# Two stacked transformer blocks on one core: modulation from transposed weights on VectorE, row broadcasts as transposes, float32 gate products over four row strips

## The chip, the cores and the metric

One Trainium2 chip, one of its cores. The metric is the device time of one execution in microseconds (us), the median of several runs of the kernel. The trace is of one more execution, taken by the hardware profiler. Engine names in the rows: PE is TensorE's matmuls, PEld its weight loads, DVE is VectorE, ACT is ScalarE, POOL is GpSimd, SP is SyncE, which issues most DMAs.

## The reference, cut to what matters

The kernel computes two blocks one after the other over a sequence of 512 tokens with 1024 columns. The first block is an FFN, a mixer (attention and a state-space part), a second FFN and a gated per-layer embedding (PLE). The second block has two layers; each modulates its input by a condition vector, runs two recurrent branches (RG-LRU and mLSTM) and projects back. What the change touches:

```python
def rms_norm(x, g):      # in every stage: one factor per token
    return x * lax.rsqrt(jnp.mean(x * x, axis=-1, keepdims=True) + EPS) * g

c_act = jax.nn.silu(c)                                    # (1, 1024)
for l in range(DEPTH_2):                                  # two layers
    mod = c_act @ w_ada[l] + b_ada[l]                     # (1, 3072)
    shift, scale, gate = jnp.split(mod, 3, axis=-1)
    h = rms_norm(x, norm_g[l]) * (1.0 + scale[:, None, :]) + shift[:, None, :]
    ...
    gates = (jnp.concatenate([q, k, v], axis=-1) @ w_if + b_if)   # in the mLSTM branch: 8 gate rows
    ...
    h = h * lax.rsqrt(jnp.mean(h * h, axis=-1, keepdims=True) + EPS)   # per head of 256 columns
    ...
    x = x + gate[:, None, :] * y
```

All of it is in float32.

## The kernel before, in words

Activations lie transposed: a tile is 128 columns of the model by 512 tokens, so a matrix of 1024 columns is eight tiles. Big matmuls take float32 numbers as a high and a low part and add three products (`mm3`, lines 125 to 127). Weights stream from memory in chunks of eight 128 x 128 blocks, in the order of use (`Stream`); each chunk is loaded by SP, its high part is copied by ScalarE (line 96) and its low part subtracted by VectorE (line 98), up to two chunks ahead. The program writes out the order of the work on each engine by hand; engines run their own instructions in order and wait for each other by semaphores.

*Row broadcasts.* A norm has one factor per token, and tokens lie along the free axis. `Norm.colsums` (line 165) sums squares over partitions with matmuls against ones, `rsqrt` (lines 207 to 214) computes the factors on VectorE as a column `col` of 128 x 4, and `Norm.part2` turns that column into a 128 x 512 tile with the factors repeated on all partitions (line 195): four matmuls, the column broadcast as the stationary operand and the identity `k.ident` as the moving one. ScalarE copies the result to SBUF (line 199). There are eight such norms. In each mLSTM head, `head_f2` does the same with the head's factors (line 1737) and VectorE multiplies two tiles by it (line 1740): four heads in each of two layers. The attention part already has transposes by TensorE (line 1023, eight of them, float32, 128 x 128).

*Modulation.* `second_prepare` makes a list of steps, each with a planned cost in us, for work that isn't needed until the second block. `Fill.grant` pops steps from that list whenever the second FFN has issued a stretch of its matmuls: 5.2 us x 0.26 of credit for each of the 44 projections, and a share after most output tiles. `silu_c` loads the condition vector as 128 x 8 and applies silu. For each layer 24 loads (`load`, 512 KB each, on SP's queue, three buffers) and 24 steps `acc` follow: VectorE multiplies the weights by the condition and adds up over the eight row blocks, four instructions over 256 columns per step (lines 1223 and 1225), into the tile `adaa` of 128 x 12 x 256. `colsum` then adds up over partitions with eight one-column matmuls against ones (line 1232), three times per layer. For layer 0 these calls are steps of the list as well; for layer 1 they are kept in `k.tail` and issued by `ple` after its last projection (`tail[0]`), by `between` before and after the broadcast of the norm in front of layer 0 (`tail[1]`, `tail[2]`), and `tail[3]` adds the bias behind the modulated tiles. `fold` (line 1245) prepares weights for the gates in the same list.

*Between PLE and layer 0.* `between` computes the norm, broadcasts it, and `modulate` makes the eight input tiles of the layer: a product with the row (lines 1350 and 1352), scale and shift on ScalarE (line 1359, high part) and VectorE (line 1360), and the low part (line 1363). Layer 1 starts by `renorm` in the same way.

*Gate products.* In `layer`, `gate_mm` (line 1479) adds the products for the eight mLSTM gates into one PSUM bank `G`, in strips of 32 rows. Per head, `qkv` issues four products of float32 parts (F32R, from `L.gvr`) into strip 0 and, after the head's q, k and v projections, four float32 products (two of q, two of k). The float32 ones go round strips 1, 2, 3 by their number `n`, sixteen in a layer. `gates1` adds the strips up with `sel8`, which has ones in every strip.

Of the kernel before, what the change touches and what calls it, by code (L numbers as in the profile page):

```python
# [129 lines left out]
class Norm:  # L130
# [60 lines left out]
    def part2(self):  # L191
        k, nc = self.k, self.k.nc
        pb = k.ps.tile([128, T], F32, name="pm", bufs=2)
        for j in range(4):
            nc.tensor.matmul(pb[:, j * 128:(j + 1) * 128], self.col[:, j:j + 1].to_broadcast([128, 128]),  # L195
                             k.ident, start=True, stop=True)
        self.wide = pb
        self.row = k.work.tile([128, T], F32, name="nrow", bufs=1)
        nc.scalar.activation(self.row, pb, AF.Copy)
# [977 lines left out]
def second_prepare(k, pool, ins):  # L1177

    nc, v = k.nc, k.nc.vector
    steps = []  # L1180
    k.lay = [Ctx() for _ in range(2)]
    c = pool.tile([128, 8], F32, name="b2c")
    th = pool.tile([128, 8], F32, name="b2cth")

    def silu_c():
        nc.sync.dma_start(c, ins["cvec"])
        nc.scalar.activation(th, c, AF.Tanh, scale=0.5)
        v.tensor_scalar(th, th, 0.5, 0.5, op0=OP.mult, op1=OP.add)
        v.tensor_mul(c, c, th)
    steps.append((0.4, silu_c))  # L1190

    for l in range(2):
        L = k.lay[l]
        L.mod = k.const2.tile([128, 24], F32, name=f"mod{l}")
        L.gs = k.const2.tile([128, 8], F32, name=f"gs{l}")
        L.sp = k.const2.tile([128, 2, 8], F32, name=f"sp{l}")
        L.hg = k.const2.tile([128, 8], F32, name=f"hg{l}")
        L.gv = k.const2.tile([128, 8, 32], F32, name=f"gv{l}")
        L.gvr = k.const2.tile([128, 8, 32], F32R, name=f"gvr{l}")
        L.wif = k.const2.tile([128, 24, 32], F32, name=f"wif{l}")  # L1200
        L.bif = k.const2.tile([128, 8], F32, name=f"bif{l}")
        L.v = lambda name, l=l: k.vec[:, VEC[f"{name}.{l}"][0]:VEC[f"{name}.{l}"][0] + VEC[f"{name}.{l}"][1]]

        def loads(L=L, l=l):
            nc.sync.dma_start(L.wif, ins["wif"][l])
            nc.sync.dma_start(L.bif, ins["bif"][l])
            nc.gpsimd.memset(L.gv, 0.0)
        steps.append((0.1, loads))

        boxes, box = {}, {}  # L1210

        def load(i, l=l, boxes=boxes):
            boxes[i] = pool.tile([128, 4, 256], F32, name="adaw", bufs=3)
            nc.sync.dma_start(boxes[i], ins["wada"][l, i // 2, :, i % 2 * 4:i % 2 * 4 + 4])

        def acc(i, boxes=boxes, box=box):
            if i == 0:
                box["a"] = pool.tile([128, 12, 256], F32, name="adaa")
            a, w = box["a"][:, i // 2], boxes[i]
            for d in range(4):  # L1220
                cd = c[:, i % 2 * 4 + d:i % 2 * 4 + d + 1]
                if i % 2 or d:
                    v.scalar_tensor_tensor(a, w[:, d], cd, a, op0=OP.mult, op1=OP.add)  # L1223
                else:
                    v.tensor_scalar(a, w[:, d], cd, None, op0=OP.mult)

        def colsum(n, L=L, box=box):

            if n == 0:
                L.mps = k.ps.tile([128, T], F32, name="pc", bufs=2)  # L1230
            for j in range(8 * n, 8 * n + 8):
                nc.tensor.matmul(L.mps[:, j:j + 1], box["a"][:, j // 2, j % 2 * 128:j % 2 * 128 + 128], k.ones[:, :1],
                                 start=True, stop=True)

        def wload(n, l=l, box=box):
            box["wv"] = pool.tile([128, 2, 2, 256], F32, name="wvt")
            nc.sync.dma_start(box["wv"], ins["wvt"][l, 2 * n:2 * n + 2].rearrange("h p a b -> p h a b"))

        def fold(n, L=L, box=box):
            ps = k.ps.tile([128, T], F32, name="pc", bufs=2)  # L1240
            for h in range(2):
                for di in range(2):
                    i = 2 * h + di
                    for do in range(2):
                        nc.tensor.matmul(ps[:, i * 8:i * 8 + 8], box["wv"][:, h, do, di * 128:(di + 1) * 128],
                                         L.wif[:, 16 + 4 * n + 2 * h + do, 0:8], start=do == 0, stop=do == 1)
            v.tensor_copy(L.gv[:, 4 * n:4 * n + 4, 0:8], ps[:, 0:32].rearrange("p (a b) -> p a b", b=8))
            if n:
                nc.scalar.activation(L.gvr, L.gv, AF.Copy)
                v.tensor_sub(L.gvr[:, :, 8:16], L.gv[:, :, 0:8], L.gvr[:, :, 0:8].bitcast(F32))  # L1250

        step = lambda cost, f, *a: steps.append((cost, lambda: f(*a)))
        for i in range(3):
            step(0.1, load, i)
        step(0.1, wload, 0)
        for i in range(24):
            step(1.4, acc, i)
            if i < 21:
                step(0.1, load, i + 3)
            if l == 0 and i in (9, 17):  # L1260
                step(0.1, colsum, i // 16)
            if i % 12 == 7:
                step(0.3, fold, i // 12)
                if i < 12:
                    step(0.1, wload, 1)

        def mods(L=L):
            v.tensor_add(L.mod, L.mps[:, 0:24], L.v("b_ada"))
            v.scalar_tensor_tensor(L.gs, L.mod[:, 8:16], 1.0, L.v("norm_g"), op0=OP.add, op1=OP.mult)
            v.tensor_scalar(L.hg, L.v("ml_norm_g"), 0.5, None, op0=OP.mult)  # L1270
        if l == 0:
            step(0.3, lambda: None)
            step(0.1, colsum, 2)
            steps.append((0.6, mods))
        else:
            k.tail = [lambda n=n: colsum(n) for n in range(3)] + [mods]

        def sp1(L=L, box=box):
            n, t = (pool.tile([128, 8], F32, name=f"spl{x}", bufs=2) for x in "ab")
            lam = L.v("rg_lambda")  # L1280
            v.tensor_scalar(n, lam, -1.0, None, op0=OP.mult)
            v.tensor_tensor(t, n, lam, op=OP.min)
            v.tensor_scalar(n, n, 0.0, None, op0=OP.max)
            nc.scalar.activation(t, t, AF.Exp)
            box["n"], box["t"] = n, t

        def sp2(L=L, box=box):
            o = pool.tile([128, 8], F32, name="splo")
            log1p_small(k, pool, box["t"], o, [128, 8], "spl1")
            v.tensor_add(o, o, box["n"])  # L1290
            v.tensor_scalar(L.sp[:, 0], o, 4.0, None, op0=OP.mult)
            v.tensor_scalar(L.sp[:, 1], o, -8.0, None, op0=OP.mult)
        steps += [(0.3, sp1), (2.0, sp2)]
    return steps


def ple(k, pool, xs, norm, pt, on_tile, early):
# [35 lines left out]
        if m:  # L1333
            gate1(m, pgs[m])
    proj(7)
    k.tail[0]()
    gate2(7, pps[7])
    early()

# [31 lines left out]
def between(k, scr, nf, ng):  # L1371
# [10 lines left out]
    v.scalar_tensor_tensor(ms, nf.ms, 1e-6, ng.ms, op0=OP.mult, op1=OP.add)  # L1382
    ng.col = k.work.tile([128, 4], F32, name="ncol", bufs=2)
    rsqrt(k, ng.col, ms)
    k.tail[1]()
    ng.part2()
    k.tail[2]()
    xs = modulate(k, 0, ng, gg, scr)
    k.tail[3]()
    rsqrt(k, nf.col, nf.ms)  # L1390

    def root():
# [19 lines left out]
def layer(k, l, xs, aside, ins, scr, norm):  # L1412
# [4 lines left out]
    with ExitStack() as st:  # L1417
# [55 lines left out]

        def gate_mm(w, x):

            parts = x.dtype == F32R
            n = ng[parts]
            g = 0 if parts else 1 + n % 3
            nc.tensor.matmul(G[g * 32:g * 32 + 32], w, x, start=n < (1 if parts else 3),
                             stop=n >= (15 if parts else 13), tile_position=None)  # L1480
            ng[parts] += 1

        def high(src, name):
# [249 lines left out]
        def head_f2(h):  # L1733
            r = S.pop(("r", h))
            ps = k.ps.tile([128, T], F32, name="pc", bufs=2)
            for t in range(4):
                nc.tensor.matmul(ps[:, t * 128:(t + 1) * 128], r[:, t:t + 1].to_broadcast([128, 128]), k.ident,
                                 start=True, stop=True)
            for m in (2 * h, 2 * h + 1):
                v.tensor_mul(n2[m], n2[m], ps)  # L1740

# [313 lines left out]
def pack(inputs, order):  # L2055
# [58 lines left out]
            a = g[n + "_2"][l]  # L2114
            mats[f"{n}.{l}"] = a.reshape(DM, a.shape[-1])
    A["pT"] = c(g["p"][0, 0].T)
    A["cvec"] = c(g["c_2"][0].reshape(8, 128).T)
    A["wada"] = c(g["w_ada_2"].reshape(2, 8, 128, 12, 256).transpose(0, 3, 2, 1, 4))
    wif = np.zeros((2, 128, 24, 32), np.float32)
    wif[..., :8] = g["ml_w_if_2"].reshape(2, 24, 128, 8).transpose(0, 2, 1, 3)  # L2120
    A["wif"] = wif
# [23 lines left out]
    "xT": (DM, T), "vecs": (128, NV), "ident": (128, 128), "wpack": (NCHUNKS, 128, CH * 128),  # L2145
    "rope": (128, 2, T), "s5n": (128, 3, 32), "s5q": (128, 3, 128), "s5cst": (128, 16),
    "s5bn": (128, 2, 512), "s5cn": (128, 2, 512), "s5bq": (8, 128, 2, 256), "s5d": (16, 32),
    "pT": (256, T), "cvec": (128, 8), "wada": (2, 12, 128, 8, 256), "wif": (2, 128, 24, 32), "bif": (2, 128, 8),
    "wvt": (2, 4, 128, 2, 256), "onehot": (8, 4, 128), "osgn": (8, 2), "sel8": (128, 8),
    "cpe": (128, 2, 16), "cw2": (128, 2, 2, 128), "ii": (124, 64), "cmask": (128, 4, 2, 32), "bglu": (128, 4),  # L2150
}
# [21 lines left out]
```

## Time and profile before

| what | value |
|---|---|
| median of 3 runs | 2014.44 us (2013.72 to 2014.51) |
| the profiled execution | 2013.55 us |
| its span, first to last instruction | 2011.8 us |
| mean granted TensorE clock | 0.98 of 2.4 GHz |
| TensorE matmuls busy | 1957.6 us, 97% of the span |
| VectorE busy | 1335.3 us, 66% |
| ScalarE busy | 815.5 us, 41% |
| bytes moved by DMA | 239.59 MB, mean 119 GB/s |

Busy time is the share of the span in which an engine worked on an instruction. A granted clock of 1.0 is TensorE's 2.4 GHz and 0.5 is 1.2 GHz; a value between is a mean over a stretch with both. A row of the timeline gives the start within the span, the length, the engine, the line of the kernel, the operation, what is written from what, and how many instructions of that kind followed each other; matmul lengths overlap, so the distance between starts tells what one costs in a stream. A float32 matmul that isn't a transpose stands in the trace as two instructions.

### The profile page before, as it was taken

How to read it: one execution, taken by the hardware profiler on the slowest of the kernel's cores; microseconds unless marked ns; L12 is line 12 of the kernel's file. 1: busy time of each engine (PE TensorE's matmuls, PEld its weight loads, DVE VectorE, ACT ScalarE, POOL GpSimd, SP SyncE). 2: the span in 40 equal slices, each digit the busy share in tenths (PEclk: the TensorE clock that was granted, in tenths of full speed). 3: DMA queues.
4: the chain of work that ended last, by engine and by line, in shares of the span. 5: the costliest groups of instructions: out<-in, count | busy, mean ns of one | idle time of the engine just before them, and what ended most of it. 6: DMA issues, size and time to landing. Idle time of an engine off the chain costs nothing. (4 is left out here: it accounts for less than half of the span.)

```text
span 2011.8 us, 24981 instructions
## 1 busy us (share of the span) xinstructions
PE 1957.6 (97%) x9432; PEld 1603.7 (80%) x9432; DVE 1335.3 (66%) x2241; ACT 815.5 (41%) x1227; POOL 161.7 (8%) x219
## 2 busy tenths in 40 slices
PE   8999999997999999999999999999999899999997
PEld 6888888886767888888888787888888677888886
DVE  7766576678655577667666775877753765777733
ACT  5323233435554332323244355555532454455521
POOL 1000000210242100000001100110000100101000
PEclk9999999998999999999999799999999899999998
DMA  5334545455201455364532143222242142232241
GB/s 186 102 117 156 160 130 154 162 189 163 90 7 37 155 183 194 118 224 168 168 104 88 45 152 115 71 88 84 74 147 95 63 157 95 74 95 84 81 139 53
DMA packets 100377, 239.59 MB, mean 119 GB/s; under 512 B 24600, under 2 KB 35608, under 8 KB 100256
## 3 DMA queue, kind: packets, MB, share of 16 engines
q1 hardware_dynamic: 100112, 237.82, 36.4%
q8 instruction: 74, 1.21, 0.2%
q14 instruction: 47, 0.39, 0.1%
q10 hardware_dynamic: 144, 0.17, 0.0%
HBM read 215.67 MB, written 21.10 MB: 118 GB/s over the span
## 5 line engine op out<-in xcount | busy, mean ns | idle before, releaser
L98 DVE TENSOR_TENSOR wlo<-wstage,whi 128x1024 fp32r<-128x1024 f32 (+1 forms) x305 | 376.0, 1240 | 149.4 <-ACT whi L96 148.9
L96 ACT ACTIVATE whi<-wstage 128x1024 fp32r<-128x1024 f32 (+1 forms) x306 | 313.5, 1043 | 142.8 <-PE pasecond L126 36.1
L277 ACT ACTIVATE t<-t 128x512 f32<-128x512 f32 x44 | 27.8, 632 | 176.9 <-DVE t L276 176.9
L1223 DVE SCALAR_TENSOR_TENSOR adaa<-adaw,b2c,adaa 128x256 f32<-128x256 f32 x168 | 81.3, 484 | 5.1
L127 PE MATMUL pahead<-xnh,wlo 128*128 128x512 f32 x208 | 81.4, 391 | 2.8 <-DVE wlo L98 2.8
L125 PE MATMUL pahead<-xnh,whi 128*128 128x512 f32 x208 | 83.4, 401 | 0.0
L153 POOL TENSOR_TENSOR nacc<-nacc,nsq 128x512 f32<-128x512 f32 x20 | 26.8, 1342 | 682.0 <-ACT nsq L149 682.0
L126 PE MATMUL pahead<-xnl,whi 128*128 128x512 f32 x208 | 81.0, 390 | 0.0
L125 PE MATMUL pbhead<-xnh,whi 128*128 128x512 f32 x192 | 77.6, 404 | 0.0
L125 PE MATMUL pbfirst<-xnh,whi 128*128 128x512 f32 x176 | 70.4, 400 | 7.1 <-ACT whi L96 6.5
L126 PE MATMUL pbhead<-xnl,whi 128*128 128x512 f32 x192 | 76.0, 396 | 0.0
L127 PE MATMUL pbhead<-xnh,wlo 128*128 128x512 f32 x192 | 76.0, 396 | 0.0
L1454 DVE SCALAR_TENSOR_TENSOR conv<-cpad,vec,conv 128x512 f32<-128x512 f32 x96 | 72.2, 752 | 5.6
L126 PE MATMUL pbfirst<-xnl,whi 128*128 128x512 f32 x176 | 69.6, 395 | 0.3 <-DVE xnl L223 0.3
L127 PE MATMUL pbfirst<-xnh,wlo 128*128 128x512 f32 x176 | 69.1, 393 | 0.0
L125 PE MATMUL pasecond<-xnh,whi 128*128 128x512 f32 x176 | 69.0, 392 | 0.0
L125 PE MATMUL pbsecond<-xnh,whi 128*128 128x512 f32 x176 | 68.8, 391 | 0.0
L125 PE MATMUL pafirst<-xnh,whi 128*128 128x512 f32 x176 | 68.7, 390 | 0.0
L127 PE MATMUL pafirst<-xnh,wlo 128*128 128x512 f32 x176 | 68.6, 390 | 0.0
L127 PE MATMUL pasecond<-xnh,wlo 128*128 128x512 f32 x176 | 68.6, 390 | 0.0
L126 PE MATMUL pafirst<-xnl,whi 128*128 128x512 f32 x176 | 68.5, 389 | 0.0
L127 PE MATMUL pbsecond<-xnh,wlo 128*128 128x512 f32 x176 | 68.5, 389 | 0.0
(754 smaller groups left out, 5266.7 us busy)
## 6 DMA issues: line engine op xcount, KB each, us to landing
wstage<-in_wpack_dram SPq DMA_DIRECT2D x304, 512.0 KB, 3.7
adaw<-in_wada_dram SPq DMA_DIRECT2D x48, 512.0 KB, 4.8
scr_v<-vv SPq DMA_DIRECT2D x16, 256.0 KB, 2.1
vr<-scr_v SPq DMA_DIRECT2D x16, 256.0 KB, 4.4
xr<-scr_x SPq DMA_DIRECT2D x16, 256.0 KB, 5.9
h<-in_xT_dram SPq DMA_DIRECT2D x8, 256.0 KB, 5.8
s5vw<-scr_wq SPq DMA_DIRECT2D x64, 32.0 KB, 2.0
s5vb<-in_s5bq_dram SPq DMA_DIRECT2D x8, 256.0 KB, 2.7
```

Of the source, the lines that this page charges most:

```text
L96: k.nc.scalar.activation(hi[:, s], st[:, s], AF.Copy)
L98: eng.tensor_sub(lo[:, s], st[:, s], hi[:, s].bitcast(F32))
L125: mm(ps, w[0], x[0], start=start, stop=False)
L126: mm(ps, w[0], x[1], start=False, stop=False)
L127: mm(ps, w[1], x[0], start=False, stop=stop)
L153: k.nc.gpsimd.tensor_add(self.acc[1], self.acc[1], sq)
L277: nc.scalar.activation(t1, t1, AF.Silu)
L1223: v.scalar_tensor_tensor(a, w[:, d], cd, a, op0=OP.mult, op1=OP.add)
L1454: v.scalar_tensor_tensor(c, xp[:, 1 + j:1 + j + T], w(j), c, op0=OP.mult, op1=OP.add)
```

## The change

Three things, in one edit:

1. `second_prepare` loads the condition vector as a row of 1024 on all 128 partitions and applies silu to all of it. The modulation weights are laid out transposed on the host: a load brings 128 output columns (as partitions) by 1024 inputs, 512 KB as before. `acc` becomes one `tensor_tensor_reduce`: product with the condition, sum along the free axis, starting from the bias, into one column of `L.mod`; the products themselves go to a tile that nobody reads. `colsum` goes, with the calls in the list, in `ple` and in `between`; `mods` loses its addition and becomes a step of the list for both layers.
2. The row broadcasts of `part2` and `head_f2` are `transpose` calls with the same operands.
3. The float32 gate products go round strips 0 to 3. Strip 0 then holds them on top of the F32R products, so only the first F32R product starts that strip.

```diff
@@ Norm.part2 @@
-            nc.tensor.matmul(pb[:, j * 128:(j + 1) * 128], self.col[:, j:j + 1].to_broadcast([128, 128]),
-                             k.ident, start=True, stop=True)
+            nc.tensor.transpose(pb[:, j * 128:(j + 1) * 128], self.col[:, j:j + 1].to_broadcast([128, 128]), k.ident)
@@ second_prepare @@
-    c = pool.tile([128, 8], F32, name="b2c")
-    th = pool.tile([128, 8], F32, name="b2cth")
+    c = pool.tile([128, DM], F32, name="b2c")
+    th = pool.tile([128, DM], F32, name="b2cth")
 
     def silu_c():
-        nc.sync.dma_start(c, ins["cvec"])
+        src = ins["cvec"]
+        nc.sync.dma_start(c, bass.AP(tensor=src.tensor, offset=src.offset, ap=[[0, 128], [1, DM]]))
...
-    steps.append((0.4, silu_c))
+    steps.append((2.4, silu_c))
...
         def load(i, l=l, boxes=boxes):
-            boxes[i] = pool.tile([128, 4, 256], F32, name="adaw", bufs=3)
-            nc.sync.dma_start(boxes[i], ins["wada"][l, i // 2, :, i % 2 * 4:i % 2 * 4 + 4])
-
-        def acc(i, boxes=boxes, box=box):
-            if i == 0:
-                box["a"] = pool.tile([128, 12, 256], F32, name="adaa")
-            a, w = box["a"][:, i // 2], boxes[i]
-            for d in range(4):
-                cd = c[:, i % 2 * 4 + d:i % 2 * 4 + d + 1]
-                if i % 2 or d:
-                    v.scalar_tensor_tensor(a, w[:, d], cd, a, op0=OP.mult, op1=OP.add)
-                else:
-                    v.tensor_scalar(a, w[:, d], cd, None, op0=OP.mult)
-
-        def colsum(n, L=L, box=box):
-
-            if n == 0:
-                L.mps = k.ps.tile([128, T], F32, name="pc", bufs=2)
-            for j in range(8 * n, 8 * n + 8):
-                nc.tensor.matmul(L.mps[:, j:j + 1], box["a"][:, j // 2, j % 2 * 128:j % 2 * 128 + 128], k.ones[:, :1],
-                                 start=True, stop=True)
+            boxes[i] = pool.tile([128, DM], F32, name="adaw", bufs=3)
+            nc.sync.dma_start(boxes[i], ins["wada"][l, i])
+
+        def acc(i, L=L, boxes=boxes):
+
+            junk = pool.tile([128, DM], F32, name="adaj")
+            v.tensor_tensor_reduce(out=junk, in0=boxes[i], in1=c, scale=1.0, scalar=L.v("b_ada")[:, i:i + 1],
+                                   op0=OP.mult, op1=OP.add, accum_out=L.mod[:, i:i + 1])
...
-            if l == 0 and i in (9, 17):
-                step(0.1, colsum, i // 16)
...
         def mods(L=L):
-            v.tensor_add(L.mod, L.mps[:, 0:24], L.v("b_ada"))
             v.scalar_tensor_tensor(L.gs, L.mod[:, 8:16], 1.0, L.v("norm_g"), op0=OP.add, op1=OP.mult)
             v.tensor_scalar(L.hg, L.v("ml_norm_g"), 0.5, None, op0=OP.mult)
-        if l == 0:
-            step(0.3, lambda: None)
-            step(0.1, colsum, 2)
-            steps.append((0.6, mods))
-        else:
-            k.tail = [lambda n=n: colsum(n) for n in range(3)] + [mods]
+        steps.append((0.4, mods))
@@ ple: k.tail[0]() goes; between: k.tail[1](), k.tail[2](), k.tail[3]() go @@
@@ layer, gate_mm @@
-            g = 0 if parts else 1 + n % 3
-            nc.tensor.matmul(G[g * 32:g * 32 + 32], w, x, start=n < (1 if parts else 3),
-                             stop=n >= (15 if parts else 13), tile_position=None)
+            g = 0 if parts else n % 4
+            nc.tensor.matmul(G[g * 32:g * 32 + 32], w, x, start=n == 0 if parts else 0 < n < 4,
+                             stop=not parts and n >= 12, tile_position=None)
@@ layer, head_f2 @@
-                nc.tensor.matmul(ps[:, t * 128:(t + 1) * 128], r[:, t:t + 1].to_broadcast([128, 128]), k.ident,
-                                 start=True, stop=True)
+                nc.tensor.transpose(ps[:, t * 128:(t + 1) * 128], r[:, t:t + 1].to_broadcast([128, 128]), k.ident)
@@ pack, on the host, and the shapes @@
-    A["cvec"] = c(g["c_2"][0].reshape(8, 128).T)
-    A["wada"] = c(g["w_ada_2"].reshape(2, 8, 128, 12, 256).transpose(0, 3, 2, 1, 4))
+    A["cvec"] = c(g["c_2"][0])
+    A["wada"] = c(g["w_ada_2"].reshape(2, DM, 24, 128).transpose(0, 2, 3, 1))
```

## Rows read from the trace of the kernel before

**Rows 1.** The page, part 1: busy time, share and instructions of each engine.

```profile
PE 1957.6 (97%) x9432; PEld 1603.7 (80%) x9432; DVE 1335.3 (66%) x2241; ACT 815.5 (41%) x1227; POOL 161.7 (8%) x219
```

**Rows 2.** Waits, whole span: who waited for whom, us in total, times, longest.

```profile
PE pm L195 <- DVE ncol L214: 5.6, 3, 2.3
...
PE pahead L127 <- DVE wlo L98: 2.8, 2, 1.4
...
PE pc L1737 <- DVE hr L1730: 1.7, 2, 0.8
...
ACT whi L96 <- PE pasecond L126: 36.1, 9, 4.4
```

**Rows 3.** Two stretches: length, busy us (instructions) of each engine, clock, DMA.

```profile
700.00:1025.00 325.00, 324.97 (x1494) 270.79 (x1493) 229.45 (x398) 89.28 (x107) 0.00 (x0) 1.00 0.52 172
...
1200.00:1225.00 25.00, 25.00 (x122) 19.61 (x121) 20.16 (x28) 12.93 (x21) 0.00 (x0) 1.00 0.40 124
```

**Rows 4.** Timeline of TensorE, a gate group: start, us, what.

```profile
1190.46 0.62 PE L1479 MATMUL pm<-ml_w_q,wif 128*32 128x512 f32 x1
...
1190.48 1.03 PE L1479 MATMUL pm<-ml_w_q,wif 128*32 128x512 f32 x2
1190.92 0.59 PE L1479 MATMUL pm<-ml_w_k,wif 128*32 128x512 f32 x1
...
1191.35 1.02 PE L1479 MATMUL pm<-ml_w_k,wif 128*32 128x512 f32 x2
1192.30 0.50 PE L125 MATMUL pbgates<-xnh,whi 128*128 128x512 f32 x1
```

**Rows 5.** Instructions of lines 195, 1737, 1023: ns minimum/median/maximum, first and last start.

```profile
L195 PE MATMUL pm<-ident,ncol x64: 271/276/561, 33.3 to 2002.3; 128*128 128x128 f32 x64
...
L1737 PE MATMUL pc<-ident,hr x64: 271/275/377, 1310.7 to 1901.7; 128*128 128x128 f32 x64
...
L1023 PE MATMUL pc<-ident,csm x8: 272/273/273, 555.0 to 555.7; 128*128 128x128 f32 x8
```

**Rows 6.** Timeline, a norm's broadcast in the second FFN.

```profile
704.61 1.05 PE L195 MATMUL pm<-ident,ncol 128*128 128x128 f32 x8
...
705.42 0.48 PE L125 MATMUL pbsecond<-xnh,whi 128*128 128x512 f32 x1
```

**Rows 7.** Timeline, the transposes that the kernel has.

```profile
554.98 1.04 PE L1023 MATMUL pc<-ident,csm 128*128 128x128 f32 x8
```

**Rows 8.** Timeline from PLE to layer 0, half clock.

```profile
1129.23 3.55 PE L1232 MATMUL pc<-ones,adaa 128*128 128x1 f32 x16
...
1131.58 0.16 DVE L214 SCALAR_TENSOR_TENSOR ncol<-rsa,rsy 128x4 f32<-128x4 f32 x1
...
1132.65 2.05 PE L195 MATMUL pm<-ident,ncol 128*128 128x128 f32 x8
...
1139.04 0.80 PE L126 MATMUL pagates<-xnl,whi 128*128 128x512 f32 x1 [0.50 <-DVE xnl L1363]
```

**Rows 9.** Timeline of TensorE, column sums of layer 0 in the second FFN.

```profile
760.41 1.84 PE L1232 MATMUL pc<-ones,adaa 128*128 128x1 f32 x16
762.11 0.48 PE L125 MATMUL pbsecond<-gh,whi 128*128 128x512 f32 x1
```

**Rows 10.** Three short stretches, columns as in rows 3; mind the clock.

```profile
550.00:575.00 25.00, 24.70 (x161) 17.20 (x160) 14.22 (x33) 15.46 (x44) 9.50 (x15) 1.00 0.00 1
1128.00:1130.00 2.00, 2.00 (x11) 2.00 (x11) 0.49 (x3) 0.00 (x0) 0.00 (x0) 0.50 0.00 0
1294.00:1298.00 4.00, 4.00 (x12) 3.14 (x11) 2.36 (x4) 2.66 (x4) 0.00 (x0) 0.57 0.00 0
```

**Rows 11.** The page, part 5: VectorE groups, busy us and mean ns.

```profile
L98 DVE TENSOR_TENSOR wlo<-wstage,whi 128x1024 fp32r<-128x1024 f32 (+1 forms) x305 | 376.0, 1240 | 149.4 <-ACT whi L96 148.9
...
L1223 DVE SCALAR_TENSOR_TENSOR adaa<-adaw,b2c,adaa 128x256 f32<-128x256 f32 x168 | 81.3, 484 | 5.1
```

**Rows 12.** Timeline of TensorE, the end of a head's sums in layer 0.

```profile
1292.75 1.03 PE L1718 MATMUL pc<-ones,nsq 128*128 128x1 f32 x8
```

More of the change, by code (lines that the diff above doesn't have):

```diff
@@ L1335, in ple @@
     proj(7)
-    k.tail[0]()
     gate2(7, pps[7])
@@ L1384, in between @@
     rsqrt(k, ng.col, ms)
-    k.tail[1]()
     ng.part2()
-    k.tail[2]()
     xs = modulate(k, 0, ng, gg, scr)
-    k.tail[3]()
     rsqrt(k, nf.col, nf.ms)
@@ L2147 @@
     "s5bn": (128, 2, 512), "s5cn": (128, 2, 512), "s5bq": (8, 128, 2, 256), "s5d": (16, 32),
-    "pT": (256, T), "cvec": (128, 8), "wada": (2, 12, 128, 8, 256), "wif": (2, 128, 24, 32), "bif": (2, 128, 8),
+    "pT": (256, T), "cvec": (DM,), "wada": (2, 24, 128, DM), "wif": (2, 128, 24, 32), "bif": (2, 128, 8),
     "wvt": (2, 4, 128, 2, 256), "onehot": (8, 4, 128), "osgn": (8, 2), "sel8": (128, 8),
```

## The prediction

> **What bounds the kernel now.** I read the page's busy shares first: TensorE is busy for 1957.6 of 2011.8 us, VectorE for 66% [rows 1]. Busy could still hide waiting, so next came the waits of TensorE over the whole span: the reader is to see that they are few and short, 5.6 us in three waits for the norm's column, 2.8 us for a weight split from VectorE and 1.7 us for a head's column are among the longest [rows 2]. In the stretch 700 to 1025 us, which holds the second FFN and nearly all of the modulation, TensorE is busy for 324.97 of 325 us while VectorE has 95 us free [rows 3]. So nearly everywhere a microsecond off TensorE's stream is a microsecond off the end, and work on VectorE is cover, not path. The sum is therefore a count of TensorE instructions taken out. The profiled execution took 2013.55 us, 1.75 us around its span and 0.89 us under the median of the runs, 2014.44 us; I subtract from the median.
>
> **Gate products.** Sixteen float32 products per layer, in groups of four after each head: eight groups. Each product is two instructions. In the group shown, three instructions start within 0.02 us on three strips, the next three 0.46 us later, and the fourth product, which shares a strip with the first, runs its two instructions alone, at 1191.35 and 0.43 us on; the next ordinary matmul starts 1192.30 - 1190.46 = 1.84 us after the group began [rows 4]. With four strips the fourth product rides in the first two rounds, and two rounds of 0.43 to 0.44 us go: 1.84 - 0.87 = 0.97 us. Eight groups: 8 x 0.87 = 7.0 us. Bounds: 0, if strip 0 doesn't run beside the others, and 8 x 0.9 = 7.2 above. I take 7.0, because rounds of three start as close as if they cost nothing more than one.
>
> **Row broadcasts.** Sixteen places: eight norms (64 records) and eight heads (64 records), each four matmuls of two instructions; the same view gives eight records for the eight transposes that the kernel already has, one each, not two [rows 5]. In the stream at full clock the eight instructions start at 704.61 and the next matmul at 705.42: 0.81 us [rows 6]. Those eight transposes are float32, of this size, with the same identity moving; they start from 555.0 to 555.7, 0.10 us apart, and all eight take 1.04 us [rows 5, 7]. So a broadcast becomes four instructions, 0.40 us, and 0.41 us goes. Three of the sixteen run at half clock (both layer starts and the last norm): eight instructions in 2.05 us, of which (2.05 - 0.42) / 7 = 0.23 us is the pitch [rows 8]; four fewer are worth 0.9 us. Sum: 13 x 0.41 + 3 x 0.9 = 8.0 us. Bounds: 0 if a transpose of a broadcast operand takes two passes after all, 13 x 0.81 + 3 x 2.05 = 16.7 us if it were free; I take the row of the same operation.
>
> **Modulation, TensorE's side.** The column sums of layer 0 go from the FFN's stream: three groups of 16 instructions, 760.41 to 762.11, 1.70 us each [rows 9], 5.1 us. Those of layer 1 lie between PLE and layer 0. The first group there fills a hole in which TensorE waits for VectorE anyway: 0. The second runs from 1129.23 and holds the broadcast up: its column is done at 1131.58 + 0.16 = 1131.74, the broadcast starts at 1132.65, 0.91 us later [rows 8]. I take 0.8 us of that, the rest for the handover. The third fills the wait for the first modulated tile, and the matmul behind it waits for VectorE until 1139.04 [rows 8]: 0 by itself; that wait moves up with the broadcast. What is late next there is VectorE's chain from the row to the split tile, as before. Clock: it is at half speed there already with these column sums running [rows 10], so they don't hold it up, and their absence can't lose it.
>
> **Modulation, VectorE's side.** Out go 168 multiply-adds of 0.484 us, 81.3 us [rows 11], and 24 plain products, which I leave out of the count. In come 48 multiply-and-sums over 1024 elements, an operation that the trace doesn't have. Nearest row: a two-operand pass over 1024 elements, 1.24 us [rows 11]; above, the pass and then a separate sum of the same length, 2.5 us. I take 1.3 us, 62 us in all, close to the one pass, since it reads and writes what that does. Both ends lie under VectorE's room (below, in the last rival), so either way nothing shows on the path. The first step now loads 512 KB of condition vector in place of 4 KB and works over 1024 columns on ScalarE and VectorE, some 2 us more on each, once; the load stands on SP's queue ahead of the modulation's first loads and one weight chunk. Its cover is that ScalarE's weight splits wait for TensorE to free a buffer (36.1 us in nine waits) [rows 2], so splits are ahead; without the cover it would cost those 2 us. Its planned cost rises by 2.0 us and others fall, so later steps move by about one grant of the fill (5.2 x 0.26 = 1.35 us in the code): 0. One addition per layer goes from VectorE, and layer 1's modulation is finished before PLE: 0.
>
> **Sum.** 7.0 + 8.0 + 5.1 + 0.8 = 20.9 us. About 10.6 us of it (gates, eight heads, one norm) falls inside the two layers, where TensorE waits now and then for VectorE's splits [rows 2]. A lead won before such a wait is partly given back; I take 2 us for that, a choice between 0 and the 4.5 us of those waits (2.8 + 1.7). Forecast: 2014.4 - 18.9 = 1995.5 us.
>
> **Rivals.** *Strip 0 stays apart.* It also takes the low-precision halves' products into the same rows of the same bank, and no row shows a float32 product on it beside the others. Then the groups keep four rounds: 18.9 - 7.0, 2002.5 us. Against it: strips 1 to 3 overlap though they share the bank. The Trainium skill ("TensorE: Matmul & The Clock Gate", Measured speedup vs the span model) lists a 16-tile packing, all four column strips in use, at 10.6 times; by that the fourth strip joins, and the sum would stand; no row here shows it. Chance 0.08.
>
> *A part is worth nothing for another reason* (broadcasts keep two passes, or the layers give back most of their 10.6 us to VectorE): 2014.4 - 18.9 + 8 = 2003.5 us. For it: VectorE is busy for 20.16 of 25 us among layer 0's gates [rows 3]. Against it: the waits shown there come to 4.5 us in all [rows 2]. Chance 0.14.
>
> *Transposes let the clock fall* (slower). Place: the thirteen broadcasts at full clock. For it: behind a run of small products that ends with eight one-column sums [rows 12] the granted clock fell, and dense work from 1294 to 1298 ran at a mean 0.57, 4 x 0.43 = 1.7 us lost [rows 10]; which kind of small work brings that on isn't separated. Thirteen such falls cost 22 us and the kernel ends at 2014.4 - 18.9 + 22 = 2017.5 us; it decides from eleven falls up. Against it: a transpose gap is 0.4 us, less than the 0.8 us it replaces, and the eight transposes there are lie in a stretch granted 1.00 throughout [rows 10]. The Trainium skill (same page, Part 4: PE-mode transpose) says that a transpose doesn't count as busy for the clock; by that rule every one of these gaps is idle time, which is this rival; the row with clock 1.00 doesn't bear it out for eight in a row. Chance 0.03.
>
> *The multiply-and-sum is slow* (slower as well). VectorE's room in the FFN is 325 - 229.45 + 81.3 = 177 us [rows 3, 11] for 48 of them: from 3.7 us each it is the bound, from 3.7 + 18.9 / 48 = 4.1 us the whole gain is gone, at 5 us the time is 1995.5 + 48 x 1.3 = 2058 us. Against it is the row of 1.24 us. Chance 0.03.
>
> **How the numbers follow.** The forecast's case has 0.72. About 0.2% (4 us) is what a measurement of this kernel tells from no change. All cases but the two slow ones and the rest end under 2010 us. The clock's dips come and go with where a short run of sums falls: the one shown cost 1.7 us, and a new order in time can bring or lose two, 3.4 us either way. Range: below, the full 20.9 with nothing given back, two dips gone and 3 us of the broadcasts' further bound: 2014.4 - 20.9 - 3.4 - 3 = 1987; above, strips or broadcasts without gain and two dips more: 2003.5 + 3.4, less a microsecond for having both at once, 2006. Faster 0.92, within 0.2% 0.03, slower 0.05.
>
> **What would show it.** Gates: 64 records in two rounds of four, next matmul about 0.97 us after the first; no gain if the fourth starts alone. Broadcasts: 32 records per line, four starting 0.10 us apart. The line of the column sums empty, TensorE still full from 700 to 1025 us; some 1.3 us for each multiply-and-sum. Layer 0's broadcast 0.15 us behind its column. I am wrong if TensorE shows new waits for VectorE or ScalarE in the FFN, if the granted clock drops behind transposes, or if layer spans shrink by much less than 5 us each.

## The result, and the profile after

The changed kernel takes 2001.92 us (median of 4 runs, 2000.82 to 2002.40); the kernel before takes 2014.43 us beside it (4 runs, 2013.72 to 2014.51). The ratio is 0.9938, 95% interval 0.9921 to 0.9955: 12.5 us faster, where 18.9 us were forecast. The profiled execution took 2002.4 us, its span is 2000.7 us, 11.1 us shorter than before.

The engines of the page's part 1, after:

```profile
PE 1935.6 (97%) x9272; PEld 1579.4 (79%) x9272; DVE 1309.6 (65%) x2143; ACT 816.6 (41%) x1227; POOL 160.3 (8%) x219
```

TensorE has 160 instructions fewer and VectorE 98 [rows 1]. Busy tables of three stretches, after, with the columns of [rows 3], whose first stretch is the first here:

```profile
700.00:1025.00 325.00, 323.87 (x1447) 265.84 (x1446) 204.01 (x307) 89.56 (x108) 0.00 (x0) 1.00 0.53 176
1030.00:1040.00 10.00, 7.53 (x30) 5.55 (x29) 4.34 (x7) 2.52 (x4) 0.00 (x0) 0.94 0.34 124
1040.00:1050.00 10.00, 10.00 (x40) 8.00 (x39) 5.60 (x8) 5.18 (x8) 0.00 (x0) 0.89 0.22 61
```

VectorE has 25 us less to do in the second FFN. Yet TensorE, which was idle there for 0.03 us before, is idle for 1.1 us, and for 2.5 us of the ten from 1030; the granted clock of these ten and of the ten behind them is below 1.00. The waits of TensorE, after (us in total, times, longest), name it:

```profile
PE pm L195 <- DVE ncol L213: 7.1, 3, 2.5
...
PE pahead L127 <- DVE wlo L98: 3.4, 2, 1.7
PE pasecond L125 <- ACT gh L233: 2.9, 2, 2.2
...
PE pc L1713 <- DVE hr L1706: 1.6, 2, 0.8
...
PE pasecond L126 <- DVE gl L234: 0.7, 3, 0.2
```

The layers' waits, which the forecast feared, hardly moved [rows 2]. New are two waits of `pasecond` for `gh` and three for `gl`: the halves of the gated tile, made by ScalarE and VectorE, that the FFN's output products read.

**The parts on TensorE did what they were to do.** A gate group, timeline of TensorE, after:

```profile
1189.97 0.62 PE L1455 MATMUL pm<-ml_w_q,wif 128*32 128x512 f32 x1
...
1189.99 0.62 PE L1455 MATMUL pm<-ml_w_k,wif 128*32 128x512 f32 x1
1190.42 0.59 PE L1455 MATMUL pm<-ml_w_q,wif 128*32 128x512 f32 x1
...
1190.97 0.50 PE L125 MATMUL pbgates<-xnh,whi 128*128 128x512 f32 x1
```

Four start within 0.02 us, the second round 0.45 us later, and the next ordinary matmul 1.00 us after the first, against 1.84 us [rows 4]: 0.84 us in six of the eight groups and 0.78 in the last of each layer, 6.6 us. The Trainium skill ("TensorE: Matmul & The Clock Gate", Measured speedup vs the span model) lists a packing of 16 tiles over four row and four column strips at 10.6 times; that four column strips run together, this trace shows too. The lines of the broadcasts and of the multiply-and-sum (ns minimum/median/maximum, first and last start), after:

```profile
L195 PE MATMUL pm<-ident,ncol x32: 270/273/447, 33.1 to 1990.1; 128*128 128x128 f32 x32
...
L1713 PE MATMUL pc<-ident,hr x32: 271/272/323, 1305.3 to 1890.9; 128*128 128x128 f32 x32
...
L1219 DVE CUSTOM_DVE_ANT_0 adaj<-adaw,b2c,vec x48: 1275/1277/1280, 709.4 to 1015.4; 128x1024 f32<-128x1024 f32 x48
L1219 DVE DVE_READ_ACCUMULATOR2_ANT mod<- x48: 79/83/86, 710.6 to 1016.6; 128x1 f32 x48
```

Thirty-two records a line stand where there were 64 [rows 5]. The multiply-and-sum is two instructions, 1.28 + 0.08 us; 1.3 us were forecast. One broadcast at full clock and the one at half clock ahead of layer 0, timeline, after:

```profile
704.22 0.60 PE L195 MATMUL pm<-ident,ncol 128*128 128x128 f32 x4
704.57 0.47 PE L125 MATMUL pbsecond<-xnh,whi 128*128 128x512 f32 x1
...
1133.51 0.16 DVE L213 SCALAR_TENSOR_TENSOR ncol<-rsa,rsy 128x4 f32<-128x4 f32 x1
...
1133.82 1.09 PE L195 MATMUL pm<-ident,ncol 128*128 128x128 f32 x4 [2.51 <-DVE ncol L213]
...
1139.29 0.80 PE L126 MATMUL pagates<-xnl,whi 128*128 128x512 f32 x1 [1.34 <-DVE xnl L1341]
```

From the broadcast to the next matmul it is 0.35 us against 0.81 [rows 6]; at half clock the broadcast lasts 1.09 us against 2.05 [rows 8], and the broadcast now starts 0.15 us behind its column, where it stood 0.91 us off. But the last row shows that the layer's second product starts at 1139.29, later than the 1139.04 of before: on arrival at layer 0 nothing is left of what was won until then. The second FFN runs from the start of its first `pasecond` product to the start of PLE's first `paple` product; timeline of TensorE, before, then after:

```profile
687.34 0.39 PE L125 MATMUL pasecond<-xnh,whi 128*128 128x512 f32 x1
...
1061.74 0.39 PE L125 MATMUL paple<-xnh,whi 128*128 128x512 f32 x1
```

```profile
686.94 0.39 PE L125 MATMUL pasecond<-xnh,whi 128*128 128x512 f32 x1
...
1065.20 0.40 PE L125 MATMUL paple<-xnh,whi 128*128 128x512 f32 x1
```

It took 374.40 us before and takes 378.26 us after. It should have lost three column-sum groups and a broadcast, 5.8 us. So 9.7 us are missing in that one stage, and the experiments look for them there.

**Two suspects in one stretch.** The FFN works in four parts: projections of five or six tiles, a gate for each, then the output products that read the gated tiles. The step from a part's projections to its output products is called a switch here. The timeline of TensorE from 1030 us, after, has both:

```profile
1031.05 0.39 PE L127 MATMUL pbsecond<-xnh,wlo 128*128 128x512 f32 x1
1031.28 0.39 PE L125 MATMUL pbsecond<-xnh,whi 128*128 128x512 f32 x1
1031.50 0.39 PE L126 MATMUL pbsecond<-xnl,whi 128*128 128x512 f32 x1
...
1034.50 0.39 PE L127 MATMUL pasecond<-gh,wlo 128*128 128x512 f32 x1
1034.74 0.39 PE L125 MATMUL pasecond<-gh,whi 128*128 128x512 f32 x1
1034.97 0.39 PE L126 MATMUL pasecond<-gl,whi 128*128 128x512 f32 x1
1035.20 0.40 PE L127 MATMUL pasecond<-gh,wlo 128*128 128x512 f32 x1
1037.85 0.50 PE L125 MATMUL pasecond<-gh,whi 128*128 128x512 f32 x1 [2.25 <-ACT gh L233]
1038.58 0.59 PE L126 MATMUL pasecond<-gl,whi 128*128 128x512 f32 x1 [0.23 <-DVE gl L234]
1038.96 0.63 PE L127 MATMUL pasecond<-gh,wlo 128*128 128x512 f32 x1
1039.39 0.63 PE L125 MATMUL pbsecond<-gh,whi 128*128 128x512 f32 x1
```

Matmuls on `xnh` and `xnl` follow each other at 0.227 us (this distance between starts is the pitch), those on `gh` and `gl` at 0.233; of the latter the second FFN has 528. Then TensorE waits 2.25 us at the switch, and the next matmuls come at 0.43 us. What kept `gh` stands in the timelines of ScalarE and of SP's queue, after:

```profile
1032.03 0.63 ACT L233 ACTIVATE pp0h<-p 128x512 fp32r<-128x512 f32 x1 [4.76 <-DMA p<-in_pT_dram]
1033.46 0.63 ACT L233 ACTIVATE pp1h<-p 128x512 fp32r<-128x512 f32 x1 [0.80 <-DMA p<-in_pT_dram]
1035.78 0.63 ACT L276 ACTIVATE t<-t 128x512 f32<-128x512 f32 x1 [1.69 <-DVE t L275]
1037.17 0.63 ACT L233 ACTIVATE gh<-t 128x512 fp32r<-128x512 f32 x1 [0.76 <-DVE t L278]
...
1027.98 0.90 SPq L1986 DMA_DIRECT2D p<-in_pT_dram  x2
```

The last steps of the fill load and split PLE's input `p`. The load is issued at 1027.98, the split waits for it until 1032.03, and behind it in ScalarE's order stands the last gate. Before, the load was issued 6 us earlier, and the same split ran without a wait:

```profile
1022.01 0.90 SPq L2011 DMA_DIRECT2D p<-in_pT_dram  x2
...
1026.54 0.61 ACT L234 ACTIVATE pp0h<-p 128x512 fp32r<-128x512 f32 x1
```

### The profile page after: what moved, and what is told of

It is laid out like the page before. It is cut to its first block, busy times and chain, and to the rows that moved or that the text cites. A ratio compares the mean times of both kernels' runs of the same rounds, so it can differ in the third digit from the quotient of the medians.

```text
span 2000.7 us, 24584 instructions
## 1 busy us (share of the span) xinstructions
PE 1935.6 (97%) x9272; PEld 1579.4 (79%) x9272; DVE 1309.6 (65%) x2143; ACT 816.6 (41%) x1227; POOL 160.3 (8%) x219
## 5 line engine op out<-in xcount | busy, mean ns | idle before, releaser
L126 PE MATMUL pbsecond<-xnl,whi 128*128 128x512 f32 x176 | 68.5, 389 | 0.0
```

The lines of the kernel that those rows point to most:

```text
L126: mm(ps, w[0], x[1], start=False, stop=False)
```

## The experiments

Three theories went in. *Order*: a fill step that lands just ahead of a part's last gate holds up VectorE or ScalarE; the planned (declared) cost of the new first step moved the steps. *Address*: the new buffers are 64 bytes a partition smaller in sum (two tiles grow from 32 to 4096 bytes, the product tile of 4096 comes, `adaa` of 12288 goes), so the tiles of the second FFN and of PLE, allocated behind them, moved by 64 bytes, and the pitch of the matmuls on `gh` and `gl` rose with it. *Rivals*: the multiply-and-sum by itself disturbs TensorE, or the layers gave the gain back. Ratios are to the kernel before, run beside on the same chip (its median there was 2014.7 to 2016.5 us); "the stretch" is the one above, first `pasecond` to first `paple`, from the timeline of each run.

| run | median us | ratio [95%] | the stretch, us |
|---|---|---|---|
| before, after (first profiles) | 2014.43, 2001.92 | 0.9938 [0.9921, 0.9955] | 374.40, 378.26 |
| a_addr | 2000.94 | 0.9924 [0.9911, 0.9936] | 373.76 |
| a_due | 1998.43 | 0.9909 [0.9896, 0.9923] | 373.84 |
| a_both | 1999.67 | 0.9913 [0.9899, 0.9926] | 372.54 |
| b_addr | 2017.30 | 1.0003 [0.9994, 1.0012] | 377.71 |
| b_addr128 | 2017.16 | 1.0010 [1.0001, 1.0020] | 377.57 |
| b_gates | 2009.14 | 0.9968 [0.9957, 0.9980] | 374.42 |
| b_trans | 2009.96 | 0.9971 [0.9960, 0.9982] | 374.01 |
| b_mod | 2015.80 | 1.0002 [0.9993, 1.0012] | 377.30 |
| b_mod_both | 2011.62 | 0.9978 [0.9969, 0.9988] | 371.46 |
| a_again | 2002.19 | 0.9939 [0.9927, 0.9951] | 378.19 |
| a_defer | 1998.83 | 0.9921 [0.9909, 0.9933] | 371.70 |
| a_best | 1995.44 | 0.9902 [0.9889, 0.9916] | 368.37 |

The expected times below were set against the 2014.4 us of the first comparison; the kernel before took 0.3 to 2.1 us more beside the runs. So hold the ratio times 2014.4 against them: `a_addr` 1999.1, `a_due` 1996.1, `a_both` 1996.9, `b_addr` 2015.0, `b_gates` 2008.0, `b_trans` 2008.6, `b_mod` 2014.8, `b_mod_both` 2010.0 us. By that, `a_addr`, `b_gates`, `b_mod` and `b_mod_both` lie in their ranges, `a_due` 0.3 us under its own, and `a_both`, `b_addr` and `b_trans` miss theirs. `a_defer` and `a_best` are held against `a_again`.

The stretch is the sharper measure. The clock dips at other places in each profile: adding up, over a profile, what consecutive ordinary matmuls (lines 125 to 127) that start 0.36 to 0.46 us apart have over 0.227 us gives 8.8 to 16.6 us in these fourteen, 11.0 before and 14.0 after; at most 1.9 us of that lies in the stretch.

**The address.** `GAPS` holds bytes left free ahead of a stage's tiles. `a_addr` is the changed kernel with

```diff
-GAPS = {..., "ple": 192}
+GAPS = {..., "ple": 256}
```

> The changed kernel with 64 bytes more left free ahead of the tiles of the per-layer embedding, so that the tiles of the second FFN and of the embedding (gh, gl, pp0h, pp1h) stand again at the SBUF addresses they had before the change. Theory (the change moved those tiles by 64 bytes, and TensorE reads a moving tile at the new address at a pitch of 393 ns instead of 389 ns): the groups of L125/L126 pasecond<-gh and <-gl go back to 389 ns, some 560 matmuls of about 6 ns, 3.4 us: 1998.4 us, between 1997.5 and 1999.5. Rival (the pitch rose because VectorE's multiply-and-sum reads SBUF beside it): the pitch stays at 393 ns and the time at 2001.9 us, within 0.8 us.

`b_addr` is the kernel before with `"ple": 128`, `b_addr128` with `"ple": 64`.

> The kernel before the change with nothing but the same tiles moved by 64 bytes the other way (64 bytes less left free), to the addresses they have after the change; instructions and their order are the same. Theory of the address: pasecond's matmuls on gh and gl go from 389 to 393 ns and the kernel takes 3.4 us more, 2017.8 us, between 2016.8 and 2018.8. Rival (no effect of the address): 2014.4 us within 0.6 us.

> The kernel before the change with the tiles moved by 128 bytes in place of 64 (128 bytes less left free than before); nothing else. If the pitch depends on whether a moving tile starts on a multiple of 128 bytes, pasecond's matmuls on gh and gl keep 389 to 391 ns and the stretch from the first pasecond to the first paple matmul keeps 374.4 us. If any move off the old place costs, or the tiles' distance to others does, they take 395 ns as with 64 bytes, and the stretch takes 377.7 us.

Groups of TensorE from 690 to 1020 us, busy us and mean ns; before:

```profile
L127 PE MATMUL pasecond<-gh,wlo 128*128 128x512 f32 x68 | 26.5, 389 | 0.0
```

`b_addr`, then `b_addr128`, then `a_addr`:

```profile
L127 PE MATMUL pasecond<-gh,wlo 128*128 128x512 f32 x68 | 26.8, 395 | 0.0
```

```profile
L125 PE MATMUL pasecond<-gh,whi 128*128 128x512 f32 x68 | 26.8, 394 | 0.0
```

```profile
L127 PE MATMUL pasecond<-gh,wlo 128*128 128x512 f32 x68 | 26.5, 389 | 0.0
```

The pitch follows the address in both directions, with the multiply-and-sum and without it: its rival falls. The matmuls of the same stage on `xnh` and `xnl`, whose tiles did not move, keep 0.227 us in all these runs, and PLE's 48 matmuls on `pp0h` to `pp1l`, which moved as well, take 0.233 us after and in `b_addr`, 0.227 before and in `a_addr`: so it is the moving operand's place. In the stretch the move costs 377.71 - 374.40 = 3.3 us. `a_addr` won more, 4.5 us, because the dip of the clock after 1037 did not come this time (the wait ahead of it did). `b_addr128` shows that it is not a matter of multiples of 128 bytes: a move by that much costs 3.2 us as well. The run as a whole is another matter. `b_addr` was to take 3.4 us more and took 0.6 us more (-1.2 to +2.4), which is its rival's time; `b_addr128` took 2.0 more (0.2 to 4.0). The stretch lost 3.3 and 3.2 us, so the verdict rests on the pitch and the stretch. Something else came out shorter in the timed runs of `b_addr`, or longer in those of the kernel before, which was profiled at the first comparison only; which, isn't shown.

**The order.** `a_due` puts back one declared cost, `a_both` adds the 64 bytes:

```diff
-    steps.append((2.4, silu_c))
+    steps.append((0.4, silu_c))
```

> The changed kernel with one number of the plan put back: the first modulation step is declared at 0.4 us as before instead of 2.4; the instructions are the same. Theory (the declared cost shifts the later steps by one grant, so that the load of the embedding's p is issued 6 us later, its split blocks ScalarE ahead of the last gate's SiLU, and TensorE waits near 1036 and loses its clock after it): p lands before its split needs it, the waits of pasecond for gh and gl near 1036 to 1039 go, the granted clock of 1030:1050 is 1.00: 4.5 us less, 1997.4 us, between 1996.4 and 1998.8. Rival (TensorE waits there because one multiply-and-sum of 1.28 us stands in VectorE's way for longer than a piece of 0.48 us did): the wait stays in some form and the time is 2001.9 us within 1 us.

> The changed kernel with both edits, the 64 bytes and the declared cost of 0.4 us. Theory: the two causes lie in different instructions and add up, 3.4 + 4.5 = 7.9 us less than 2001.9: 1994.0 us, between 1992.5 and 1996. If the layers had given back the gain instead (rival), nothing of the kind happens ahead of the layers and the time stays above 2000 us.

In `a_due` the wait near 1035 is gone, with its dip, and the delays near 759 too; the stretch is 4.4 us shorter, though at the switch near 860 `gh` came 1.5 us late instead of 0.2. But the two causes did not add up in `a_both`: 7.9 us were expected, and its stretch is 5.7 us shorter. The delay at the switch near 860 grew to 2.0 us there, which VectorE's timeline of `a_both` explains:

```profile
856.76 1.28 DVE L1219 CUSTOM_DVE_ANT_0 adaj<-adaw,b2c,vec 128x1024 f32<-128x1024 f32 x1 [3.69 <-DMA adaw<-in_wada_dram]
...
857.97 0.69 DVE L275 TENSOR_TENSOR t<-pasecond,nrow 128x512 f32<-128x512 f32 x1
```

A modulation step waits for its weights until 856.76 and then works for 1.28 us, and the last gate stands behind it (L275 starts at 857.97). TensorE's next `pasecond` product came 2.0 us late, and the clock dipped behind it for 1.6 us. So the load of `p` was one case of something more general: whichever step stands ahead of the last gate passes its own waits on to TensorE. With the declared cost at 2.4 that hits the switches near 759, 861 and 1035, with 0.4 the one near 860. `a_defer` tests that by itself: the changed kernel, all numbers as they are, where the last grant of a part comes behind the gate.

```diff
-                    k.fill.grant(5.2 * rate)
+                    if not (k.phase == "second" and i and f == f0 + n - 1):
+                        k.fill.grant(5.2 * rate)
                 if f == 0:
                     first = pp
                 else:
                     gate(*pp)
+                if k.phase == "second" and f == f0 + n - 1:
+                    k.fill.grant(5.2 * rate)
```

> The changed kernel as it is, so that it stands on the same chip as the next two. Both theories expect the ratio to before of the first comparison, 0.994 within 0.002, and 378.3 us from the first pasecond matmul to the first paple matmul, give or take 2 us for a dip of the clock there.

> The changed kernel with one edit of order: in the second FFN the last gate of each of the four parts is put on the engines ahead of the grant of modulation steps, not behind it. Theory (a modulation step put just ahead of the last gate holds VectorE or ScalarE while TensorE waits for that gate's gh and gl): the excess ahead of pasecond<-gh at the part switches, 0.83 + 0.49 us near 759, 0.49 near 861, 2.42 + 0.50 near 1035, falls below 0.3 us in all places, and the clock's dip after 1037 (1.7 us) with it: 373 us from the first pasecond to the first paple matmul, 4 to 6 us less than the changed kernel in the same call. Rival (the multiply-and-sums are too long for VectorE wherever they stand, or the late load of p alone is to blame): excesses of 0.5 us and more stay at two or more of the switches, and less than 3 us is won.

> The changed kernel with all three: that order, the 64 bytes given back, and the first step declared at 0.4 us. Theory: the second FFN gets what the change should have brought it, 374.4 - 5.1 - 0.5 = 368.8 us from the first pasecond to the first paple matmul, at most 370.5; 8 to 10 us less than the changed kernel in the same call, 0.989 of before. Rival (the losses move to another place when these are taken away): 373 us or more in that stretch.

The last switch, timeline of TensorE in `a_best`:

```profile
1030.86 0.39 PE L127 MATMUL pasecond<-gh,wlo 128*128 128x512 f32 x1
1031.09 0.39 PE L125 MATMUL pasecond<-gh,whi 128*128 128x512 f32 x1
1031.50 0.50 PE L126 MATMUL pasecond<-gl,whi 128*128 128x512 f32 x1
```

In `a_defer` and `a_best` no matmul on `gh` or `gl` at a switch starts more than 0.19 us late; in `a_best` the matmuls on `gh` are at 0.227 us again. `a_defer` takes 378.19 - 371.70 = 6.5 us out of the stretch, `a_best` 3.3 us more: 368.37 us, where 368.8 were expected. With the order right, the declared cost seems worth nothing: the step from `a_defer` to `a_best`, which changes both, is the address's 3.3 us. `a_best` is faster than both kernels: 1995.44 us (1993.03 to 1997.47) against 2002.19 (2002.03 to 2004.19) for the changed kernel on the same chip. That is 6.8 us of the stretch's 9.8, where 8 to 10 were expected. In `a_defer` 3.4 of 6.5 us arrive, where 4 to 6 were expected; part of the rest is seen in layer 0, which took 3.9 us longer there than in `a_again` (1.9 in `a_best`). Granted clock (the number behind the instructions) of TensorE in two places of layer 0, `a_defer`, then the same two in `a_again`, where the layer starts 5.3 us later:

```profile
1330.00:1340.00 10.00, 9.49 (x39) 0.83 0.32 105
1390.00:1400.00 10.00, 8.71 (x33) 0.67 0.50 158
```

```profile
1335.00:1345.00 10.00, 10.00 (x52) 1.00 0.34 105
1395.00:1405.00 10.00, 9.10 (x46) 1.00 0.49 158
```

The instructions of the layer are the same; the dips are not (`a_again` has one behind 1291, which `a_defer` lacks). What places them wasn't tested.

**Parts alone.** Each is the kernel before with one part of the change's diff: strips (`b_gates`), transposes in both places (`b_trans`), modulation (`b_mod`), and modulation with 256 and 0.4 in the two numbers above (`b_mod_both`).

> The kernel before the change with the gate products over four row strips and nothing else. Theory: the group goes from 1.84 to 1.00 us eight times, 6.7 us less, all inside the two layers, and nothing of it is given back: 2007.7 us, between 2007 and 2009.5. Rival (the layers give part of it back to VectorE's splits): 2010 us or more, with new waits of the layers' matmuls for weight splits.

> The kernel before the change with the two row broadcasts as transposes and nothing else. Theory: 13 x 0.46 us at full clock and 3 x 0.96 us at half clock, 8.9 us less: 2005.5 us, between 2004.5 and 2008. Rival (transposes let the clock fall or the heads wait for VectorE's column sooner): 2009 us or more, with the granted clock below 1.00 behind the broadcasts in more places than before.

> The kernel before the change with the modulation part alone (multiply-and-sum from transposed weights, no column sums, the first step declared at 2.4 us). Theory: 5.1 + 0.8 us of column sums go, and the moved addresses (3.4 us) and the late load of p (about 4.5 us) come: 2.0 us slower than before, 2016.4 us, between 2013.5 and 2018. Rival (the losses belong to another part, or to the parts together): 5.9 us less, 2008.5 us.

> The modulation part alone, with the 64 bytes given back and the first step declared at 0.4 us. Theory: the part's own worth without its two side effects, 5.1 + 0.8 us: 2008.5 us, between 2007.5 and 2010.5. Rival (the multiply-and-sums cost TensorE something by themselves, as long pieces on VectorE): 2011 us or more, with waits of pasecond for VectorE at the part switches of the FFN.

The strips bring 6.4 us (4.0 to 8.7, by the ratio on 2014.4 us): as expected. The transposes bring 5.8 us (3.6 to 8.1), less than the 8.9 expected. In the profile the thirteen broadcasts at full clock won 0.45 to 0.56 us each and those at the two layer starts, at half clock, 0.96; but from layer 0's heads to its output the stage took 0.4 us longer instead of 1.9 shorter, with 1.2 us more of dips than before. The rest of what is missing isn't traced. The modulation alone brings nothing (0.4 us slower, -1.4 to +2.4): the rival's 2008.5 us is excluded, and its stretch of 377.3 us shows the waits and the pitch without the other two parts. Without its side effects' two numbers it brings 4.4 us (2.4 to 6.2), short of 5.9: the wait near 860 came there too, with `gh` 2.0 and `gl` 0.5 us late. Such a wait is what this run's rival had named, so the run alone doesn't exclude it; `a_defer` does, where the same 48 multiply-and-sums stand behind the last gates and delay none.

## Why the prediction was right and wrong

The sign, the range and the mechanism on TensorE were right; the gain is a third smaller than forecast, because one step priced at 0 cost 6.5 us and another, for which the sum has no term, 3.3 us. That the time lies in the range is in part luck: the room above was left for strips or broadcasts without gain and for two more dips, and none of these used it up.

| term of the sum | forecast | measured |
|---|---|---|
| gate products | -7.0 | 6 x 0.84 + 2 x 0.78 = -6.6 |
| broadcasts | -8.0 | 13 x 0.48 + 3 x 0.96 = -9.1 |
| column sums in the FFN | -5.1 | 3 x (1.70 + 0.09) = -5.4 |
| between PLE and layer 0 | -0.8 | -1.1 |
| given back in the layers | +2 | +0.4 |
| order of the fill's steps | 0 | +6.5 |
| tiles moved by 64 bytes | no term | +3.3 |
| landing of the last store | no term | +1.1 |
| rest, not traced | | -0.2 |
| sum | -18.9 | -11.1 |

- *Gates.* Right, strip 0 joins. The rival in which it stays apart fell.
- *Broadcasts.* Right in kind. At full clock each was worth 0.45 to 0.56 us (0.48 on average), not 0.41: most take 0.35 us to the next matmul instead of the 0.40 that the pitch of the eight suggested, and some had taken 0.91 us, not 0.81.
- *Column sums.* Right. The 0.09 us, which the step left out, is that behind a group the second ordinary matmul starts 0.32 us after the first, not 0.227.
- *Between.* From the last PLE product to layer 0's second product the path is 2.1 us shorter; less the broadcast's 0.96, that is 1.1 us.
- *Given back.* From layer 0's second product to layer 1's second product the time shrank by 6.1 us, from there to the issue of the last output store by 6.3, with as much dipping as before (7.9 us by the sum above). The parts by the sizes measured come to 12.8 us (gates 6.6, heads 3.8, three norms 2.4; the prediction counted one norm there), so 0.4 us were given back. The choice of 2 was too high, and the wrong stage was feared.
- *The last store.* The eight output stores took 2.0 us each from issue to landing before; after, the slowest took 3.0. Before, then after:

```profile
DMA to landing us min/median/max: 2.0/2.0/2.0
```

```profile
DMA to landing us min/median/max: 2.0/2.0/3.0
```

The span ends 1.0 us behind that landing in both, so 1.1 us of it went there. That isn't the change's doing: with the changed kernel's instructions it is 3.2 us in `a_again` and `a_addr`, 2.0 in `a_due`.
- **The step that failed**: "Its planned cost rises by 2.0 us and others fall, so later steps move by about one grant of the fill [...]: 0." The steps did move, and that was taken for free. But a grant puts its steps ahead of the last gate in the engines' order, so it matters what each of them waits for. The load and split of `p` and a multiply-and-sum landed there. The prediction asked whether VectorE has room on the whole (it has, 121 us in the stretch from 700) and named new waits of TensorE for VectorE or ScalarE in the FFN as what would make it wrong, which came; it did not look at which steps stand ahead of the four gates that TensorE waits for. `a_defer` changes nothing but that, and gains 6.5 us in the stretch.
- **The step that was missing**: buffers change size, so tiles behind them move. No term was written for it. It cost 3.3 us in 528 matmuls (`b_addr`).
- *The rival "a part is worth nothing"*, at 2003.5 us, is nearer to the measured 2001.92 than the forecast, and in kind it came: the modulation alone brought nothing (`b_mod`). But neither reason that it named (two passes, the layers) was the cause.
- *Clock.* The rival that transposes let it fall did not come: in the 8 us behind each of the thirteen broadcasts at full clock the granted clock is 1.00, in the profile of the changed kernel and in that of `b_trans`. The Trainium skill ("TensorE: Matmul & The Clock Gate", Part 4: PE-mode transpose) says that a transpose doesn't count as busy for the clock in the same way; four of them in 0.35 us cost no clock here. In the second FFN it fell anew after 1037, where TensorE had waited 2.25 us for data.
- *The slow multiply-and-sum.* At 1.28 + 0.08 us it is far from the 3.7 us that would make VectorE the bound.

With both side effects taken away, `a_best` stands 19.7 us (16.9 to 22.4) under before by its ratio, about where the prediction had put the change itself (18.9, or 20.9 with nothing given back).

## What to carry to other kernels

Work that is handed out "when there is room" is placed in an engine's order, and there it passes on whatever it waits for. Before pricing a moved step at nothing, list the few instructions that a full TensorE waits for (the last gate of each part, here) and see which steps stand just ahead of them; put the grant behind them. And when a change resizes a buffer, compare the addresses of all tiles allocated behind it, and the pitch of the matmuls that read them: run the old kernel with nothing but that move.

## What was not expected of the hardware

- The pitch of a 128 x 512 float32r matmul depends on where its moving tile lies: 0.227 us at the old place, 0.233 us with the tiles 64 or 128 bytes lower, 6 ns each. What in the address decides stays open; only these three places were tried, and multiples of 128 bytes don't explain it.
- The multiply-and-sum shows as two instructions, 1.28 us and a read of the accumulator, 0.08 us. The Trainium skill ("VectorE: DVE Perf Modes", Two Vector instructions with no wait between them) says that an operation which also writes out its accumulator is two instructions; the trace agrees, and prices the sum beside the product at next to nothing: the plain two-operand pass over as many elements takes 1.24 us [rows 11].
- A pause of TensorE near 1035 was followed by a dip of the clock in both profiles of the changed kernel (2.25 and 2.39 us; in the first, 0.94 and 0.89 in the two windows above), and by none in those of `a_addr` and `b_mod` (2.46 and 2.40 us); the pause alone does not decide it.
- The last of eight output stores, alike in all profiles, landed 2.0 us after its issue in ten of the fourteen and 3.0 to 3.2 us after it in four.
